# Where the inputs of four convolution pairs are kept: two pairs move from the mixers' pool to the pool that outlives it

## The chip, the cores and the metric

The kernel runs on one core of one Trainium2 chip. The metric is the device time of one launch in microseconds (us), the median of the runs shown. Lower is better. The engines are named as in the profile: PE (TensorE), with PEld for its weight loads, DVE (VectorE), ACT (ScalarE), POOL (GpSimd) and SP (SyncE, which here only issues DMAs).

## The reference, cut to what matters

One decoder layer on a sequence of 1024 positions with 1024 channels, all in float32. The part that matters here is the Conformer branch and what runs beside it:

```python
def conformer_branch(u_glu, dw_w, dw_b, ln_g, ln_b, w_out):
    a, g = jnp.split(u_glu, 2, axis=-1)
    v = a * jax.nn.sigmoid(g)
    v = causal_dwconv(v, dw_w, dw_b)          # 31 taps, each channel by itself
    v = jax.nn.silu(layer_norm(v, ln_g, ln_b))
    return v @ w_out
...
    y_a = conformer_branch(...)
    y_b = ssd_branch(...)
    h = LN(alpha*h + (sigmoid(gate_a)*y_a + sigmoid(gate_b)*y_b) @ w_o)
    h = LN(alpha*h + conv_ffn(h))
```

The convolution at a position needs the 30 positions before it, so the end of the first half of the sequence is needed again at the start of the second.

## The kernel before, in words

The sequence is worked through in two halves of 512 positions (`hh` 0 and 1). Each half runs `mixers(hh)`, then `combine(hh)`, then an output projection; the feed-forward part follows for both halves together. Activations lie with channels on the 128 partitions, so a tile of 128 channels and 512 positions is one matmul wide.

**Products in three parts.** Every float32 product is three matmuls on rounded parts (`mm3`, lines 183 to 185): high weights by high input, high weights by low input, low weights by high input. `project` (line 187) does this for 8 slices of 128 input channels, 24 matmuls for one output tile. `weights` (line 144) brings the weights: SP loads 512 KB into a tile `st` (line 147, 3 buffers), ACT casts it to the high part of `w` (line 149, 3 buffers), and DVE subtracts to get the low part (line 154, called the split below). The first matmuls of line 183 and 184 need only the cast; line 185 needs the split.

**mixers(hh)** has four groups. In each group `glu` (line 434) makes two tiles `v` of the convolution's input, `v = a * sigmoid(g)` with 30 columns of the previous half in front (line 443 copies them from `v_halo`; line 446 saves the end of the half there). Then `conv31` (line 449) works on the pair: ACT makes the start value `c` (line 455), and DVE adds 30 taps for each tile, one SCALAR_TENSOR_TENSOR each (line 466). Group g has the tiles i = 2g and 2g+1: the first pair is v0 and v1, the fourth v6 and v7. The taps have the lowest priority (`high_priority(offset=-1500)`), so the taps of the fourth pair are done during `combine`. `c` of the first six is stored to DRAM; c6 and c7 stay in the memory of the core.

**combine(hh)** does eight rounds. Each round has a projection for the second gate (`gate`, weights `w_gb`, sigmoid on ACT in line 739) and one for the second half of the state-space output (`w_sp`), with `mb = (ya + ps) * gb` on DVE (lines 759 and 760; `ya` is loaded by SP in line 750 as `yb`). On PE the order is gb0, gb1, sp0, gb2, sp1, gb3, sp2, gb4 and so on. Beside that the layer norm of the convolution's output is made: POOL sums the eight `c` (lines 699 and 701), a float32 matmul with `mean_w` gives the mean (line 706, in `deviations`), DVE subtracts it (line 708), ACT squares, POOL sums (line 714), a second such matmul gives the variance (line 718).

**What sets the order.** Nobody writes the order of an engine's instructions by hand. A scheduler orders them at build time by priority and by its own model of when an instruction could run and when a tile's memory is free. Once built, each engine takes its instructions in that order and waits on semaphores. So a change of where a tile lies can change the order around it.

**Pools.** `statep` ("states") is opened before the first half and closed after the second `combine`. `pl` in `mixers` is opened anew for each half, and the pool of `combine` takes over its memory when it closes. The tiles `v` lie in `pl`, with 4 buffers; v4 takes the place of v0, and v6 that of v2.

Of the kernel before, what the change touches and what calls it, by code (L numbers as in the profile page):

```python
# [8 lines left out]
F32 = mybir.dt.float32  # L9
# [7 lines left out]
P = 128  # L17
D = 1024
T = 1024
HALF = 512  # L20
# [3 lines left out]
KC = 31  # L24
# [31 lines left out]
def kernel(  # L56
# [18 lines left out]
    def pool(name, bufs=1, **kw):  # L75
        return tc.tile_pool(name=name, bufs=bufs, reuse_waits="tile", **kw)
# [11 lines left out]
    def bank(which):  # L88
        n_ps[0] += 1
        pl, tag = (pacc, "acc") if which else (psm, "sm")  # L90
        return pl.tile([P, 512], F32, tag=tag, name=f"{tag}{n_ps[0]}")
# [4 lines left out]
    statep = state_stack.enter_context(pool("states", side="right"))  # L96
# [65 lines left out]
    def col_weights(hh, ct):  # L162
        scr = low_scr.get(ct)
        return weights(
            wcol[ct], f"c{hh}_{ct}", None if hh else scr, scr if hh else None
        )
# [20 lines left out]
    def project(ps, w, xs):  # L187
        for k in range(KD):
            mm3(
                ps,  # L190
                lambda i: w[:, i, k * P : (k + 1) * P],
                lambda i: xs[:, i, k, :],
                k == 0,
                k == KD - 1,
            )
# [238 lines left out]
    def glu(pl, hh, hT, i):  # L434
        pa, pg = bank(1), bank(1)
        wa = col_weights(hh, CT_A + i)
        project(pa, wa, hT)
        wg = col_weights(hh, CT_G + i)
        project(pg, wg, hT)
        v = pl.tile([P, HALF + KC - 1], F32, tag="v", bufs=4, name=f"v{hh}_{i}")  # L440
        s = pl.tile([P, HALF], F32, tag="sig", name=f"sig{hh}_{i}")
        A.activation(out=s, in_=pg, func=AF.Sigmoid)
        A.copy(v[:, : KC - 1], v_halo[:, i, :])
        V.tensor_mul(v[:, KC - 1 :], pa, s)
        if hh == 0:
            A.copy(v_halo[:, i, :], v[:, HALF:])
        return v
# [195 lines left out]
    def mixers(hh, hT):  # L643
        pre = first_columns(hh, hT, (CT_B, CT_C, CT_X))
        with pool(f"mixers{hh}") as pl:
            time_steps(pl, hh, pre[0])
            scaled = parts = None
            for g in range(GROUPS):
                BT = conv4(pl, hh, column(hh, hT, CT_B + g) if g else pre[1], 16 + g)
                CT = conv4(pl, hh, column(hh, hT, CT_C + g) if g else pre[2], 20 + g)  # L650
                xT = pl.tile([P, 4, HALF], F32, tag="x4", bufs=2, name=f"x4_{hh}_{g}")
                for i in range(4):
                    j = 4 * g + i
                    conv4(pl, hh, column(hh, hT, CT_X + j) if j else pre[3], j, xT[:, i, :])
                zs = z_gate(pl, hh, hT, g)
                vs = [(i, glu(pl, hh, hT, i)) for i in (2 * g, 2 * g + 1)]
                if g:
                    scaled()
                if g == 1:
                    yT = big_tile(f"yT{hh}_0")  # L660
                if g in (1, 2):
                    parts(yT)
                split_2 = parts
                scaled, parts = ssd_group(pl, hh, g, xT, BT, CT, zs)
                if g == 3:
                    ssm_out_first(pl, hh, yT)
                    yT = big_tile(f"yT{hh}_2")
                    split_2(yT)
                    gate_first(pl, hh, hT, range(3))
                    scaled()  # L670
                    parts(yT)
                with tc.high_priority(offset=-1500):
                    accs = conv31(pl, hh, vs)
            gate_first(pl, hh, hT, range(3, 8))
# [531 lines left out]
    mixT, _ = combine(1, hT, yT, accs)  # L1206
# [122 lines left out]
```

## Time and profile before

| what | value |
|---|---|
| three runs | 1958.3, 1958.61, 1961.29 us; median 1958.61 us |
| the profiled execution | 1960.26 us, its span 1958.4 us |
| granted PE clock, mean over the span | 0.997 |
| PE busy | 1929.1 us, 99% of the span |
| DVE busy | 1599.8 us, 82% |
| ACT busy | 1081.2 us, 55% |
| POOL busy | 218.9 us, 11% |

The span is the part of the profiled execution between its first and last instruction; 1.86 us of its time lie outside. A row of the timeline reads: start in us from the span's start, duration, engine, line, operation, output<-inputs, shape, count, and in brackets how long the engine sat idle just before and what released it. Rows of equal instructions that follow each other are merged, so a row x11 lasts from its start to the end of the eleventh. Names in the profile have no buffer numbers: `w_gb` is any of the gates' weight tiles.

### The profile page before, as it was taken

The page shows a single profiled execution, that of the slowest core. Times are in us where ns is not written, and L with a number is a line of the kernel's source. Part 1 is how long each engine was busy: PE and PEld are TensorE (multiplying, and loading weights), DVE is VectorE, ACT ScalarE, POOL GpSimd, SP SyncE. Part 2 cuts the span into 40 slices and gives each one's busy share as a digit, 9 for nine tenths or more (in the row PEclk, how much of TensorE's full clock was granted, in tenths as well). Part 3 has the DMA queues.
Part 4 walks back from the last instruction along what each step waited for, and adds up shares of the span by engine and source line. Part 5 has one row for each costly group of instructions (what it writes and reads, how often), then busy time and mean ns, then how long its engine had stood idle before and what let it go on. Part 6 is the DMA issues. An engine that isn't in the chain of part 4 may idle for free.

```text
span 1958.4 us, 25837 instructions
## 1 busy us (share of the span) xinstructions
PE 1929.1 (99%) x9453; PEld 1574.9 (80%) x9453; DVE 1599.8 (82%) x2224; ACT 1081.2 (55%) x1615; POOL 218.9 (11%) x258
## 2 busy tenths in 40 slices
PE   9999999999999999999999999999999999989997
PEld 8888878788788788888878888888888888867886
DVE  7599999999786538898999546587788888879778
ACT  4676767653263266777765435365555555544432
POOL 0001010112210001111112140010000000121010
PEclk9999999999999999999999999999999999999999
DMA  7645555447355565556545644566455455588673
GB/s 270 224 166 205 174 202 185 159 171 245 116 188 212 198 214 175 205 181 208 176 159 168 216 145 134 188 237 230 163 167 189 166 188 178 198 301 276 195 230 127
DMA packets 127648, 378.36 MB, mean 193 GB/s; under 512 B 15104, under 2 KB 15648, under 8 KB 127520
## 3 DMA queue, kind: packets, MB, share of 16 engines
q1 hardware_dynamic: 107424, 318.48, 48.2%
q0 software_dynamic: 13760, 46.69, 6.9%
q10 hardware_dynamic: 6336, 11.54, 1.6%
q8 instruction: 74, 1.21, 0.3%
q14 instruction: 54, 0.44, 0.1%
HBM read 289.99 MB, written 86.65 MB: 192 GB/s over the span
## 4 chain that ended last, share of the span: by engine, by line
PE 60%; DVE 10%; DMA 3%; ACT 2%; issue 2%; DVEq 0%; SPq 0%; ACTq 0%
PE acc L185 13%; PE acc L184 13%; PE acc L183 13%; PE sm L184 6%; PE sm L185 6%; PE sm L183 6%; DVE c L466 4%; DMA dr<-wdown 1%; DVE x L421 1%; DMA st_wo<-wo 1%; DMA b_scr<-fo 1%; PE sm L551 1%; PE sm L554 0%; DVE m L546 0%; ACT m L519 0%
## 5 line engine op out<-in xcount | busy, mean ns | idle before, releaser
L183 PE MATMUL acc<-hT,w_c 128*128 128x512 f32 x1000 | 391.2, 391 | 0.0
L185 PE MATMUL acc<-hT,w_c 128*128 128x512 f32 x1000 | 391.1, 391 | 0.0
L184 PE MATMUL acc<-hT,w_c 128*128 128x512 f32 x1000 | 391.0, 391 | 0.0
L466 DVE SCALAR_TENSOR_TENSOR c<-v,pc,c 128x512 f32<-128x512 f32 x480 | 369.7, 798 | 7.3 <-ACT c L455 4.5
L183 PEld LDWEIGHTS acc<-hT,w_c 128*128 128x128 f32 x1000 | 187.8, 188 | 40.6 <-issue 1.9
L185 PEld LDWEIGHTS acc<-hT,w_c 128*128 128x128 f32 x1000 | 187.8, 188 | 40.0 <-issue 1.5
L184 PEld LDWEIGHTS acc<-hT,w_c 128*128 128x128 f32 x1000 | 187.8, 188 | 39.5 <-issue 1.1
L149 ACT CAST w_c<-st_c 128x1024 fp32r<-128x1024 f32 x128 | 133.9, 1046 | 127.6 <-PE acc L185 100.6
L530 POOL TENSOR_TENSOR ce<-ce,xbc 128x1024 f32<-128x1024 f32 x28 | 82.2, 2936 | 681.7 <-ACT ce L529 681.7
L1116 ACT CAST w_dn<-dr 128x1024 fp32r<-128x1024 f32 (+1 forms) x73 | 68.6, 944 | 88.3 <-DMA dr<-wdown 36.7
L183 PE MATMUL sm<-h1s,w_s 128*128 128x512 f32 x264 | 102.7, 389 | 0.0
L184 PE MATMUL sm<-h1s,w_s 128*128 128x512 f32 x264 | 102.7, 389 | 0.0
L185 PE MATMUL sm<-h1s,w_s 128*128 128x512 f32 x264 | 102.2, 389 | 0.0
L519 ACT ACTIVATE m<-ab,acs 128x128 f32<-128x128 f32 x256 | 78.3, 390 | 37.7 <-PE sm L551 36.6
L154 DVE TENSOR_TENSOR w_c<-st_c,w_c 128x1024 fp32r<-128x1024 f32 x64 | 79.4, 1243 | 22.3 <-ACT w_c L149 17.1
L1117 DVE TENSOR_TENSOR w_dn<-dr,w_dn 128x1024 fp32r<-128x1024 f32 (+1 forms) x73 | 78.9, 1092 | 6.1 <-ACT w_dn L1116 6.1
L421 DVE SCALAR_TENSOR_TENSOR x<-u,pc,x 128x512 f32<-128x512 f32 x96 | 78.8, 835 | 3.9 <-ACT x L419 3.8
L185 PE MATMUL acc<-h1b,w_ue 128*128 128x512 f32 x176 | 68.8, 394 | 0.3 <-DVE w_ue L154 0.3
L183 PE MATMUL acc<-h1b,w_ue 128*128 128x512 f32 x176 | 68.7, 390 | 0.0
L184 PE MATMUL acc<-h1b,w_ue 128*128 128x512 f32 x176 | 68.5, 389 | 0.0
L183 PE MATMUL sm<-h1b,w_s 128*128 128x512 f32 x176 | 68.5, 389 | 0.0
L184 PE MATMUL sm<-h1b,w_s 128*128 128x512 f32 x176 | 68.5, 389 | 0.0
(325 smaller groups left out, 4547.3 us busy)
## 6 DMA issues: line engine op xcount, KB each, us to landing
st_c<-wcol SPq DMA_DIRECT2D x128, 512.0 KB, 4.4
low_scr<-w_c SPq DMA_DIRECT2D x64, 512.0 KB, 2.9
w_c<-low_scr SPq DMA_DIRECT2D x64, 512.0 KB, 4.4
ab<-acs_scr SPq DMA_DIRECT2D x32, 512.0 KB, 4.1
dr<-wdown SPq DMA_DIRECT2D x55, 256.0 KB, 5.2
st_wo<-wo SPq DMA_DIRECT2D x24, 512.0 KB, 4.5
st_ue<-wup SPq DMA_DIRECT2D x22, 512.0 KB, 3.6
first_scr<-first ACTq DMA_DIRECT2D x44, 256.0 KB, 3.0
```

What stands on the lines that cost most here:

```text
L149: casts.append(A.copy(w[:, 0, :], st))
L154: V.tensor_tensor(out=w[:, 1, :], in0=st, in1=w[:, 0, :].bitcast(F32), op=ALU.subtract)
L183: TE.matmul(ps, wa(0), xa(0), start=start, stop=False, skip_group_check=more)
L184: TE.matmul(ps, wa(0), xa(1), start=False, stop=False, skip_group_check=more)
L185: TE.matmul(ps, wa(1), xa(0), start=False, stop=stop, skip_group_check=more)
L421: V.scalar_tensor_tensor(out=o, in0=u[:, k : k + HALF], scalar=pc[:, wc + k : wc + k + 1], in1=o, op0=ALU.mult, op1=ALU.add,)
L466: V.scalar_tensor_tensor(out=accs[i], in0=v[:, k : k + HALF], scalar=pc[:, wc + k : wc + k + 1], in1=accs[i], op0=ALU.mult, op1=ALU.add,)
L519: A.activation(out=m[:, h, :], in_=ab[:, h, :], func=AF.Relu, scale=-1.0, bias=acs[:, c, 8 * g + h : 8 * g + h + 1],)
L530: G.tensor_tensor(out=ce, in0=ce, in1=CT[:, cs].unsqueeze(1).to_broadcast([P, 8, P]), op=ALU.mult)
L551: TE.matmul(o, xs[:, h * HP : (h + 1) * HP], m[:, h, :], start=True, stop=first)
L1116: A.copy(w[:, 0, cs], src)
L1117: V.tensor_tensor(out=w[:, 1, cs], in0=src, in1=w[:, 0, cs].bitcast(F32), op=ALU.subtract)
```

## The change

The tiles `v` of the second and fourth pair (i = 2, 3, 6, 7) are taken from `statep` with 2 buffers, those of the first and third pair (0, 1, 4, 5) from `pl` with 2 buffers. The number of tiles and all arithmetic stay. v6 still takes the place of v2. What is new is that v6 and v7 no longer lie in memory that `combine` takes over, and that v2 and v3 of the second half take the places of v6 and v7 of the first.

```diff
-        v = pl.tile([P, HALF + KC - 1], F32, tag="v", bufs=4, name=f"v{hh}_{i}")
+        v = (statep if i & 2 else pl).tile(
+            [P, HALF + KC - 1], F32, tag="v", bufs=2, name=f"v{hh}_{i}"
+        )
```

All lines behind these stand two further down in the changed kernel (line 466 becomes 468, line 706 becomes 708, line 154 stays).

On POOL the order of instructions is the same; on the other engines it differs in few places. The first is DVE in `combine` of the first half, from the split of sp1's weights on. `c_6` and `c_7` are the convolution's sums of the fourth pair, `w_gb_3`, `w_sp_2`, `w_gb_4` the weights of the next projections. Before:

```order
L154 TENSOR_TENSOR w_sp_1_4622<-st_sp_1_4620,w_sp_1_4622 128x1024
L466 SCALAR_TENSOR_TENSOR c_6_4222<-v_6_3506,pc,c_6_4222 128x512
L466 SCALAR_TENSOR_TENSOR c_7_4224<-v_7_3574,pc,c_7_4224 128x512 x10
L154 TENSOR_TENSOR w_gb_3_4654<-st_gb_3_4652,w_gb_3_4654 128x1024
L759 TENSOR_TENSOR mb_0_4528<-yb_0_4526,acc_4553 128x512
L154 TENSOR_TENSOR w_sp_2_4688<-st_sp_2_4686,w_sp_2_4688 128x1024
L760 TENSOR_TENSOR mb_0_4528<-mb_0_4528,gb_0_4492 128x512
L759 TENSOR_TENSOR mb_1_4529<-yb_1_4617,acc_4619 128x512
```

The same place on DVE in the changed kernel:

```order
L154 TENSOR_TENSOR w_sp_1_4622<-st_sp_1_4620,w_sp_1_4622 128x1024
L468 SCALAR_TENSOR_TENSOR c_6_4222<-v_6_3506,pc,c_6_4222 128x512
L468 SCALAR_TENSOR_TENSOR c_7_4224<-v_7_3574,pc,c_7_4224 128x512 x2
L761 TENSOR_TENSOR mb_0_4528<-yb_0_4526,acc_4553 128x512
L468 SCALAR_TENSOR_TENSOR c_7_4224<-v_7_3574,pc,c_7_4224 128x512
L762 TENSOR_TENSOR mb_0_4528<-mb_0_4528,gb_0_4492 128x512
L154 TENSOR_TENSOR w_gb_3_4654<-st_gb_3_4652,w_gb_3_4654 128x1024
L468 SCALAR_TENSOR_TENSOR c_7_4224<-v_7_3574,pc,c_7_4224 128x512 x4
L154 TENSOR_TENSOR w_sp_2_4688<-st_sp_2_4686,w_sp_2_4688 128x1024
L468 SCALAR_TENSOR_TENSOR c_7_4224<-v_7_3574,pc,c_7_4224 128x512 x3
L761 TENSOR_TENSOR mb_1_4529<-yb_1_4617,acc_4619 128x512
```

Seven of the ten taps of c7 moved behind the split of `w_gb_3`, and three of these behind that of `w_sp_2`; the sum and the product of `mb_0` moved ahead of the split of `w_gb_3`.

The second place is ACT in the same stage. `v_2_7066` and `v_3_7131` are tiles of the second half; in the kernel before, their copies of line 443 stand some 90 rows later, at the start of the second `mixers`. Before:

```order
L149 CAST w_sp_1_4622<-st_sp_1_4620 128x1024
L739 ACTIVATE gb_0_4492<-acc_4462 128x512
L149 CAST w_gb_3_4654<-st_gb_3_4652 128x1024
L739 ACTIVATE gb_1_4524<-acc_4494 128x512
L149 CAST w_sp_2_4688<-st_sp_2_4686 128x1024
L739 ACTIVATE gb_2_4615<-acc_4585 128x512
L149 CAST w_gb_4_4745<-st_gb_4_4743 128x1024
```

The same place on ACT in the changed kernel:

```order
L741 ACTIVATE gb_0_4492<-acc_4462 128x512
L149 CAST w_sp_1_4622<-st_sp_1_4620 128x1024
L741 ACTIVATE gb_1_4524<-acc_4494 128x512
L445 COPY v_2_7066<-v_halo 128x30
L149 CAST w_gb_3_4654<-st_gb_3_4652 128x1024
L149 CAST w_sp_2_4688<-st_sp_2_4686 128x1024
L741 ACTIVATE gb_2_4615<-acc_4585 128x512
L445 COPY v_3_7131<-v_halo 128x30
L149 CAST w_gb_4_4745<-st_gb_4_4743 128x1024
```

Two copies now stand ahead of casts. The first waits for the last tap of c6, which is the last reader of v6; the second for the last tap of c7.

The third place is PE in the same stage; `sm_4717` is the mean of the convolution's sums, `acc_4742` the projection gb4. One piece of the difference (- before, + changed):

```order
 L184 MATMUL acc_4685<-yT_2_4096,w_sp_2_4688 128x512
 L185 MATMUL acc_4685<-yT_2_4096,w_sp_2_4688 128x512
+L708 MATMUL sm_4717<-stats_4461,mean_w 128x512
 L183 MATMUL acc_4742<-hT_338,w_gb_4_4745 128x512
 L184 MATMUL acc_4742<-hT_338,w_gb_4_4745 128x512
@@ -2061,5 +2062,4 @@
 L183 MATMUL acc_4742<-hT_338,w_gb_4_4745 128x512
 L184 MATMUL acc_4742<-hT_338,w_gb_4_4745 128x512
-L706 MATMUL sm_4717<-stats_4461,mean_w 128x512
 L185 MATMUL acc_4742<-hT_338,w_gb_4_4745 128x512
 L183 MATMUL acc_4742<-hT_338,w_gb_4_4745 128x512
```

The mean's matmul moved from inside the projection gb4, where 20 of its 24 matmuls stood ahead of it, to the front of it.

Besides these: the matmul of the variance moved three matmuls forward, from inside the projection gb6 to the front of it; the loads of `yb` for mb0 and mb1 moved on SP ahead of the loads of gb3's, sp2's and gb4's weights; on DVE, four of the subtractions of line 708 moved ahead of the split of `w_gb_5`; some squares of line 713 moved on ACT against casts; and the copies of line 443 for v2 and v3 of the first half moved to the very start of ACT's instructions, where a load of an activation table now stands ahead of them. No other instruction moved.

## The prediction

> **What bounds the kernel now.** I read the page's engine rows first, then PE's waits, then the timeline around the longest of them.
>
> ```profile
> span 1958.4 us, 25837 instructions
> PE 1929.1 (99%) x9453; PEld 1574.9 (80%) x9453; DVE 1599.8 (82%) x2224; ACT 1081.2 (55%) x1615; POOL 218.9 (11%) x258
> ```
>
> PE is busy for 99% of the span. So only two things can shorten the kernel: fewer or faster matmuls, or a wait of PE that goes. The change leaves the matmuls alone. Two rows of PE's waits (us in total, times, longest):
>
> ```profile
> PE acc L185 <- DVE w_gb L154: 4.2, 1, 4.2
> PE sm L551 <- DVE m L546: 2.7, 2, 2.5
> ```
>
> The longest single wait of the kernel, 4.2 us, is on a split of gate weights, and it happens once. It lies in the first `combine`, on PE:
>
> ```profile
> 499.39 0.39 PE L183 MATMUL acc<-yT,w_sp 128*128 128x512 f32 x1
> 504.83 0.39 PE L183 MATMUL acc<-hT,w_gb 128*128 128x512 f32 x1
> 505.06 0.39 PE L184 MATMUL acc<-hT,w_gb 128*128 128x512 f32 x1
> 509.67 0.80 PE L185 MATMUL acc<-hT,w_gb 128*128 128x512 f32 x1 [4.22 <-DVE w_gb L154]
> 517.12 0.39 PE L183 MATMUL acc<-yT,w_sp 128*128 128x512 f32 x1
> ```
>
> From 499.39 to 504.83 a projection of 24 matmuls takes 5.44 us, a step of 0.227 us each. The third matmul of gb3, the first that needs the low weights, was due at 505.06 + 0.23 = 505.29 and starts at 509.67: **4.38 us** lost. The 22 steps from there to the next projection at 517.12 take 7.45 us in place of 22 x 0.227 = 4.99: another **2.46 us**. The table of stretches says why (PE busy, then the granted clock):
>
> ```profile
> 505.00:507.80 2.80, 0.44 (x2) 1.00 0.00 0
> 507.80:509.60 1.80, 0.00 (x0) 0.50 0.00 0
> 509.60:514.60 5.00, 4.93 (x12) 0.50 0.75 255
> 514.60:520.00 5.40, 5.40 (x25) 1.00 0.49 154
> ```
>
> The clock drops to half at about 507.8, in the wait, and stays there to 514.6. The place costs 4.38 + 2.46 = 6.84 us in all. What PE waits for stands on DVE:
>
> ```profile
> 497.94 1.22 DVE L154 TENSOR_TENSOR w_sp<-st_sp,w_sp 128x1024 fp32r<-128x1024 f32 x1
> 499.07 9.41 DVE L466 SCALAR_TENSOR_TENSOR c<-v,pc,c 128x512 f32<-128x512 f32 x11
> 508.39 1.22 DVE L154 TENSOR_TENSOR w_gb<-st_gb,w_gb 128x1024 fp32r<-128x1024 f32 x1
> 509.53 0.68 DVE L759 TENSOR_TENSOR mb<-yb,acc 128x512 f32<-128x512 f32 x1
> 511.75 0.68 DVE L760 TENSOR_TENSOR mb<-mb,gb 128x512 f32<-128x512 f32 x1
> 500.52 1.66 DVE L466 SCALAR_TENSOR_TENSOR c<-v,pc,c 128x512 f32<-128x512 f32 x1
> 503.00 0.75 DVE L466 SCALAR_TENSOR_TENSOR c<-v,pc,c 128x512 f32<-128x512 f32 x1
> ```
>
> The split of `w_gb_3` stands behind eleven taps, one of c6 and ten of c7. The last two rows are single taps out of the eleven. The split ends at 508.39 + 1.22 = 509.61; PE starts 0.06 us later.
>
> **The change, part by part.**
>
> *Taps behind the split.* By the order, DVE now runs the tap of c6, two taps of c7, the sum of `mb_0`, one tap, the product of `mb_0`, and then the split. The second tap of c7 is the row at 500.52 and ends at 502.18. Then come 0.68 + 0.75 + 0.68 = 2.11 us, the split starts at 504.29, ends at 505.51, and PE starts at 505.57 where it was due at 505.29. A rest of 0.28 us stays. Neighbouring rows overlap a little (509.53 + 0.68 is past the next start), so the rest could be zero. **Gain: 4.38 - 0.28 = 4.10 us.**
>
> *The clock.* A wait of 2.52 us elsewhere left the clock at full:
>
> ```profile
> 997.14 0.44 PE L551 MATMUL sm<-m,xs 128*64 128x128 f32 x4 [2.52 <-DVE m L546]
> 994.50:997.10 2.60, 0.12 (x1) 0.00 (x0) 1.63 (x3) 2.59 (x4) 0.00 (x0) 1.00 0.80 312
> 997.10:1000.50 3.40, 3.36 (x38) 2.99 (x39) 3.40 (x7) 3.37 (x6) 0.00 (x0) 1.00 0.73 241
> ```
>
> So a rest of 0.28 us should leave it there too: **gain 2.46 us**, in all 6.56. The Trainium skill, page "TensorE: Matmul & The Clock Gate", section "HAM oscillation — how this bites in real kernels", prices such a drop at half of the throttled time. By that the 6.8 us at half clock would be an estimated 3.4 us, and the gain 7.5. The rows give less, since PE sat idle for 1.9 of the 6.8 us, and I keep the rows.
>
> *The copies on ACT.* ACT is in order, so what stands behind the copy of v2 (the casts of `w_gb_3` and `w_sp_2`) waits for c6's last tap. The row of ACT's cast for gb3 before, the group of copies (ns, min/median/max), and POOL's last two sums:
>
> ```profile
> 494.15 1.06 ACT L149 CAST w_gb<-st_gb 128x1024 fp32r<-128x1024 f32 x1 [3.89 <-PE acc L185]
> L443 ACT COPY v<-v_halo x16: 198/226/234, 27.4 to 920.0; 128x30 f32<-128x30 f32 x16
> 499.96 1.67 POOL L701 TENSOR_TENSOR stats<-stats,c 128x512 f32<-128x512 f32 x1 [8.93 <-DVE c L466]
> 508.62 2.12 POOL L701 TENSOR_TENSOR stats<-stats,c 128x512 f32<-128x512 f32 x1 [6.99 <-DVE c L466]
> ```
>
> c6's tap ends at 499.07 + 0.75 = 499.82, the copy near 500.1, the cast of `w_gb_3` near 501.2: 6 us later than before, but 3 us ahead of 504.29, when DVE comes to the split, and ahead of PE's 504.83. Cost nothing; without that cover it would be 1:1. The copy of v3 waits for c7's last tap: 505.51, four taps at 0.79 (eight took 502.18 to 508.48), a split of 1.22, three taps: 512.3. Cast of `w_gb_4` by 513.6; its split follows the two `mb_1` steps, by 515 (by 516 if it takes 2.3 us beside POOL). PE reaches gb4 at 505.57 + 22 x 0.227 + 5.44 = 516.0 and needs the low weights a matmul of the mean (1 us) later. Cost nothing.
>
> *The mean's matmul.* It needs POOL's sum with c7, 2.12 us after c7's last tap: 512.3 + 0.14 + 2.12 = 514.5. In front of gb4 PE comes to it at 516.0. Margin 1.5 us. The 20 matmuls that stood ahead of it (4.5 us) are gone as cover, so a later sum would cost 1:1. Then the subtractions start 11 us earlier than before, and the split of `w_gb_5` moves behind four of them: DVE has room, as it sat idle here:
>
> ```profile
> 518.41 1.22 DVE L154 TENSOR_TENSOR w_sp<-st_sp,w_sp 128x1024 fp32r<-128x1024 f32 x1 [3.52 <-ACT w_sp L149]
> 528.16 3.68 DVE L708 TENSOR_TENSOR cc<-cc,sm 128x512 f32<-128x512 f32 x6 [2.85 <-PE sm L706]
> 543.41 0.56 POOL L289 DMA_DIRECT2D in_sq<-gin  x1 [0.30 <-POOL stats L714]
> 545.89 1.02 PE L718 MATMUL sm<-stats,mean_w 128*128 128x512 f32 x2
> ```
>
> POOL's last sum of squares ended 0.3 us before 543.41, 15 us after 528.16. From 517 that is 532, and PE comes to the variance at about 538.6 (545.89 less the gain and three matmuls). Cost nothing.
>
> *Loads on SP.* The two `yb` loads now go ahead of the load of `st_gb_3`:
>
> ```profile
> 480.14 0.43 SPq L641 DMA_DIRECT2D g_scr<-gt  x1
> 486.52 0.33 SPq L147 DMA_DIRECT2D st_gb<-wcol  x1
> 499.61 0.85 SPq L750 DMA_DIRECT2D yb<-y_scr  x2
> ```
>
> SP is free from 480.6 to 486.5, and issuing both takes 0.85 us. Nothing queues behind them.
>
> *The start.* ACT gets a table load and two copies ahead of its first square root:
>
> ```profile
> 0.80 1.28 ACT L239 ACT_TABLE_LOAD   x1 [0.80 <-PEq L1316]
> 1.91 0.29 POOL L116 MEMSET v_halo<- 128x240 f32 x1
> 6.00 0.29 ACT L239 ACTIVATE rs_in<-mv_in,eps 128x1 f32<-128x1 f32 x1 [3.92 <-DVE mv_in L238]
> ```
>
> The load ends at 2.08, `v_halo` is ready at 2.2, two copies take 0.45, a second load 1.28: done by 4.0, with 2 us of idle time left before 6.00. Cost nothing.
>
> *The sum.* 6.56 us off the profiled execution's 1960.26 gives 1953.70, span 1951.84. That execution stands 1.65 us above the median of 1958.61. If none of these 1.65 lie in this wait, the median falls to 1952.05; if all do, the median run has only 4.91 to give, and 1953.70 stays. I take **1952.5**, nearer to the first: two of the three runs lie within 0.3 us of each other, so the 1.65 may as well be of the profiled execution as a whole. What is late next is the same split, by 0.28 us.
>
> **The rivals.**
>
> *The clock still drops.* If DVE is slower here, the rest grows. Rows for it: a tap took 1.66 us beside POOL's sum, and a split took 2.31 beside POOL at 484.18, `mb` 1.07 at 535.92:
>
> ```profile
> 484.18 2.31 DVE L154 TENSOR_TENSOR w_sp<-st_sp,w_sp 128x1024 fp32r<-128x1024 f32 x1
> 535.92 1.07 DVE L760 TENSOR_TENSOR mb<-mb,gb 128x512 f32<-128x512 f32 x1
> ```
>
> With those prices on all four steps the split ends 2.8 us later, the wait is 3.1 us, and with a drop of the clock the gain is 6.84 - 3.08 - 2.46 = 1.3: **1957.3**. It decides where the wait passes about 2.5 us, where the clock fell in the row above. The same page, section "Part 1: The HAM clock gate", lets the clock fall only after an idle window of about 3.4 us, by which this rival would need a still longer wait; in this trace it fell 2.5 us in, so I go by the trace. Against it: POOL's sum ends at 501.63, before these steps. Chance 0.09.
>
> *The gain is given back.* If a later stage runs at the pace of DVE or ACT, PE only waits there instead: **1958.6**. For it: in the second `mixers` PE has the 2.52 us wait above. Against it: that is all it has there, and DVE's waits right behind the place (3.52, 2.85) end on ACT and PE, which both come earlier. Chance 0.07.
>
> *Slower: PE held by the mean.* Seven taps of c7 now lie between the split and the mean, which stands in front of gb4. Their group:
>
> ```profile
> L466 DVE SCALAR_TENSOR_TENSOR c<-v,pc,c x480: 656/750/2912, 95.8 to 1094.1; 128x512 f32<-128x512 f32 x160
> ```
>
> At the longest of 2.912 us seven taps take 20.4 in place of 5.5 us. The sum is 14.9 late, less the margin of 1.5 leaves a wait of 13.4, and the clock drops (2.46): 15.9 lost against 6.56 gained, **1968.0**. Once the clock drops, 4.10 of the gain are left, so it decides for slower where the seven taps cost over 1.5 + 4.10 us more than 5.5, about 1.6 us each. Against it: the median is 0.75, and POOL is idle in that stretch. Chance 0.04.
>
> **How the numbers follow.** My forecast, with the wait gone and the gain kept, has 0.80. All its values gain more than 3.9 us, which is 0.2% and about what a measurement of this kernel can tell from no change: faster 0.80. The first two rivals are within it: same 0.16. Slower 0.04. Low end: 6.84 off the fastest run, 1958.3, is 1951.5, less 1 us for runs that scatter by 3: 1950.5. High end: the first rival's 1957.3. What is left out above, give-back and held mean, has 0.11.
>
> **What would show it.** Right: PE's wait on `w_gb` gone from the top of its waits, or under 0.5 us; the clock at 1.00 through 505 to 520; sp2 starting near 510.6 in place of 517.12; only one split between seven taps and the mean; a span of 1951 to 1953. The copy steps are wrong if a cast of `w_gb` waits on DVE and PE behind it. The mean step is wrong if PE shows a wait on POOL at line 708. The whole is wrong if sp2 starts early and the span stays: then a new wait of PE after 520 names the place.

## The result, and the profile after

| | before | after |
|---|---|---|
| median | 1961.29 us | 1955.61 us |
| lowest to highest, 9 runs each | 1958.3 to 1967.26 us | 1952.82 to 1958.13 us |
| the profiled execution, its span | 1960.26 us, 1958.4 us | 1952.82 us, 1951.1 us |

The ratio is 0.997, with a 95% interval of 0.9961 to 0.9978. So the changed kernel is 0.3% faster: by the ratio 5.9 us of 1961, between 4.3 and 7.6 (the two medians lie 5.7 apart). The profiled execution after is the fastest of its nine. The three runs of before that the prediction worked with were the first of these nine.

The engine rows of the changed kernel's page:

```profile
span 1951.1 us, 25836 instructions
PE 1928.4 (99%) x9453; PEld 1574.6 (81%) x9453; DVE 1599.3 (82%) x2224; ACT 1082.7 (55%) x1616; POOL 217.6 (11%) x258
```

No engine has less to do than before; ACT has one table load more. The span is 7.3 us shorter because PE waits less: it is idle for 22.7 us in place of 29.3, and busy for 0.7 us less. PE's longest waits in the changed kernel (us in total, times, longest):

```profile
PE acc L184 <- DVE w_dn L1119: 2.9, 3, 1.5
PE sm L553 <- DVE m L548: 2.7, 2, 2.5
PE sm L257 <- POOL ident masks.py:199: 1.7, 1, 1.7
PE acc L183 <- ACT w_dn L1118: 1.5, 2, 1.1
PE sm L184 <- DVE w_dn L1119: 1.1, 1, 1.1
```

The wait of 4.2 us on `w_gb` is gone. The place itself on PE's timeline, from gb3 to the variance:

```profile
504.69 0.39 PE L183 MATMUL acc<-hT,w_gb 128*128 128x512 f32 x1
505.18 0.50 PE L185 MATMUL acc<-hT,w_gb 128*128 128x512 f32 x1
510.30 0.39 PE L183 MATMUL acc<-yT,w_sp 128*128 128x512 f32 x1
515.75 1.02 PE L708 MATMUL sm<-stats,mean_w 128*128 128x512 f32 x2
516.20 0.79 PE L183 MATMUL acc<-hT,w_gb 128*128 128x512 f32 x1
538.39 1.02 PE L720 MATMUL sm<-stats,mean_w 128*128 128x512 f32 x2
```

The third matmul of gb3, due two steps after 504.69 at 505.15, starts at 505.18: 0.03 us lost where it was 4.38. From gb3's first row to sp2's first row it is 5.61 us; the 24 steps take 5.44 undisturbed, so 0.17 us are lost where 6.85 were. The place has given 6.7 us. Neither the mean (515.75) nor the variance (538.39) shows a wait. DVE at the same place:

```profile
502.05 0.68 DVE L761 TENSOR_TENSOR mb<-yb,acc 128x512 f32<-128x512 f32 x1
502.65 0.74 DVE L468 SCALAR_TENSOR_TENSOR c<-v,pc,c 128x512 f32<-128x512 f32 x1
503.31 0.68 DVE L762 TENSOR_TENSOR mb<-mb,gb 128x512 f32<-128x512 f32 x1
503.91 1.21 DVE L154 TENSOR_TENSOR w_gb<-st_gb,w_gb 128x1024 fp32r<-128x1024 f32 x1
505.05 3.10 DVE L468 SCALAR_TENSOR_TENSOR c<-v,pc,c 128x512 f32<-128x512 f32 x4
508.07 1.22 DVE L154 TENSOR_TENSOR w_sp<-st_sp,w_sp 128x1024 fp32r<-128x1024 f32 x1
509.20 2.32 DVE L468 SCALAR_TENSOR_TENSOR c<-v,pc,c 128x512 f32<-128x512 f32 x3
```

The split starts at 503.91 and ends at 505.12. The prediction had 504.29 and 505.51. Each row starts 0.07 to 0.09 us before the one above it has ended: from the sum of `mb_0` to the split it is 1.86 us where the durations add up to 2.10. That is most of the 0.38 us, and so the rest of 0.28 us, which the prediction allowed might be zero, was 0.03. ACT, and POOL's sums:

```profile
499.79 0.22 ACT L445 COPY v<-v_halo 128x30 f32<-128x30 f32 x1 [9.68 <-DVE c L468]
499.92 1.05 ACT L149 CAST w_gb<-st_gb 128x1024 fp32r<-128x1024 f32 x1
511.56 0.22 ACT L445 COPY v<-v_halo 128x30 f32<-128x30 f32 x1 [9.15 <-DVE c L468]
511.68 1.05 ACT L149 CAST w_gb<-st_gb 128x1024 fp32r<-128x1024 f32 x1
```

```profile
511.67 1.30 POOL L703 TENSOR_TENSOR stats<-stats,c 128x512 f32<-128x512 f32 x1 [10.09 <-DVE c L468]
```

ACT stands idle for 9.68 and 9.15 us behind the two copies, and PE loses nothing by it: the first cast ends at 500.97, about 3 us before DVE comes to its split. The sum for the mean ends at 512.97, 2.8 us before PE needs it; the margin had been put at 1.5, with a sum of 2.12 us in place of 1.30.

The stretch around the place, in before and then in the changed kernel (us, busy us and count of PE, PEld, DVE, ACT, POOL; granted clock; DMA share; GB/s):

```profile
475.00:545.00 70.00, 65.78 (x279) 53.58 (x278) 56.48 (x59) 22.14 (x30) 24.32 (x16) 0.95 0.42 139
```

```profile
475.00:545.00 70.00, 70.00 (x306) 57.08 (x305) 61.16 (x63) 25.42 (x36) 23.52 (x16) 1.00 0.48 162
```

PE fills all 70 us and does 27 matmuls more in them, at full clock. The next 155 us, in before and then in the changed kernel:

```profile
545.00:700.00 155.00, 155.00 (x719) 126.32 (x718) 109.34 (x167) 70.63 (x104) 4.29 (x8) 1.00 0.58 201
```

```profile
545.00:700.00 155.00, 155.00 (x729) 126.36 (x728) 107.15 (x171) 70.55 (x105) 4.29 (x8) 1.00 0.58 198
```

PE stays full in both, so the gain isn't given back there.

### The profile page after: what moved, and what is told of

The parts are those of the page before. It is cut to its first block, busy times and chain, and to the rows that moved or that the text cites. A ratio compares the mean times of both kernels' runs of the same rounds, so it can differ in the third digit from the quotient of the medians.

```text
span 1951.1 us, 25836 instructions
## 1 busy us (share of the span) xinstructions
PE 1928.4 (99%) x9453; PEld 1574.6 (81%) x9453; DVE 1599.3 (82%) x2224; ACT 1082.7 (55%) x1616; POOL 217.6 (11%) x258
## 4 chain that ended last, share of the span: by engine, by line
PE 90%; DVE 5%; DMA 3%; ACT 1%; issue 1%; SPq 0%; POOL 0%; DVEq 0%; ACTq 0%
PE acc L185 21%; PE acc L183 21%; PE acc L184 21%; PE sm L184 6%; PE sm L185 6%; PE sm L183 6%; PE sm L553 2%; PE sm L561 1%; PE sm L556 1%; DMA dr<-wdown 1%; PE sm L514 1%; DMA b_scr<-fo 1%; DVE c L468 0%; PE acc L402 0%; DVE x L421 0%
```

## The experiments

All kernels here compute the whole reference. Times are medians; the ratio is to the kernel before, run on the same chip (1960.68 us in the first four experiments, 1960.47 in e5 to e8, 1960.44 in e9 and e10). Diffs are against the changed kernel. `issue_after(a, b)`, a helper of the kernel, makes the scheduler put a behind b on their engine.

My theory: the gain comes from DVE's order alone, and the pools matter only because they make the scheduler choose it. The rival: the memory itself brings it, since v6 and v7 no longer lie where `combine` takes over, or since early copies or loads help.

**e1: the new pools, with DVE's order of before.**

```diff
+                if hh == 0 and j == 3:
+                    issue_after(los[-1], tap[0, 7, KC - 2])
+                    issue_after(first_mb[0], los[-1])
...
+                if hh == 0 and j == 2:
+                    issue_after(los[-1], first_mb[0])
+                    issue_after(first_mb[1], los[-1])
```

`los[-1]` is the split just issued, `tap[0, 7, KC - 2]` the last tap of c7, `first_mb` the steps of `mb_0`. A further line keeps sp2's matmuls behind gb3's on PE.

> The changed kernel with the tiles where the change put them, but DVE made to follow the order of the kernel before at the one place: ten taps of c7, then the split of w_gb_3, then mb_0. Theory (the order of DVE at this place is the whole gain): PE waits about 4.2 us on the split again, the clock drops to half behind it, and the time is that of the kernel before within 0.1% (ratio 0.999 to 1.001). Rival (the place of the tiles in memory, or the mean and the copies that moved with them, bring the gain): ratio about 0.997, as the changed kernel.

Measured: 1961.04 us, ratio 1.0002 (0.9993 to 1.001). PE's timeline at the place:

```profile
505.70 0.39 PE L184 MATMUL acc<-hT,w_gb 128*128 128x512 f32 x1
510.61 0.79 PE L186 MATMUL acc<-hT,w_gb 128*128 128x512 f32 x1 [4.29 <-DVE w_gb L155]
518.16 0.39 PE L184 MATMUL acc<-yT,w_sp 128*128 128x512 f32 x1
```

gb3 began at 505.70 and sp2 at 518.16, so 12.46 - 5.44 = 7.02 us were lost, wait and clock together. The copies on ACT stay where the change put them (the first at 500.78, ahead of gb3's cast), and so does the mean (523.61, in front of gb4). With the memory of the change and the order of before, the whole gain is gone, to within 0.1%. So the memory alone doesn't bring it, and neither do the copies or the mean by themselves: the rival falls. The opposite trial, the pools of before with DVE's order of the change, was not run, so it isn't shown that the order would bring the gain without the new memory.

**e2: the mirror.** The first and third pair go to `statep`, the second and fourth stay in `pl`; nothing else changes, and DVE keeps its order of before.

```diff
-        v = (statep if i & 2 else pl).tile(
+        v = (pl if i & 2 else statep).tile(
```

> The mirror of the change: first and third pair in the pool that outlives the mixers, second and fourth in the mixers' pool. As many bytes change pools, but DVE keeps the order of the kernel before at the place. Theory: the 4.2 us wait stays, ratio 0.999 to 1.001. Rival (the smaller mixers' pool or the shifted addresses bring it): ratio about 0.997.

Measured: 1961.72 us, ratio 1.0009 (0.9999 to 1.0018). PE's timeline, and the stretches from the wait to sp2:

```profile
509.89 0.74 PE L185 MATMUL acc<-hT,w_gb 128*128 128x512 f32 x1 [4.13 <-DVE w_gb L154]
```

```profile
505.50:510.00 4.50, 0.37 (x3) 0.11 (x1) 4.36 (x7) 0.89 (x1) 1.15 (x1) 1.00 0.00 0
510.00:513.40 3.40, 3.40 (x8) 2.65 (x9) 3.37 (x5) 0.00 (x0) 0.97 (x1) 0.50 0.71 238
```

The same wait stands, and 6.04 us are lost at the place. As many tiles moved between the pools, and no gain: it matters which pairs move. That fits the theory: the taps that stand ahead of the split are those of the fourth pair. The clock's part was 1.75 us here and not 2.46, because the drop came only at 510.0, after the wait had ended, and lasted 3.4 us, half as long as in before.

**e3 and e4: three and five of the seven taps back ahead of the split.** This sets the wait to sizes between 0 and 4.4 us, to price the place and find where the clock falls.

```diff
+                if hh == 0 and j == 3:
+                    issue_after(los[-1], tap[0, 7, 25])
```

In e4 the number is 27 in place of 25.

> The changed kernel with three of the seven taps put back ahead of the split of w_gb_3. The split ends 3 x 0.775 = 2.3 us later, so PE waits 2.3 us there. If the clock stays at full after so short a wait, 2.3 of the 6.6 us of gain are lost in the trace and the ratio is about 0.998; if it drops, 4.8 are lost and the ratio is about 0.9993.

> The same with five of the seven taps put back: PE waits 3.9 us. If the drop of the clock is a price of its own, it comes here: 3.9 + 2.5 us lost, nearly the whole gain, ratio about 1.000. If the clock stays, 3.9 us lost, ratio about 0.9988.

Measured, e3: 1957.13 us, ratio 0.9981 (0.9972 to 0.999). e4: 1958.4 us, ratio 0.9987 (0.9978 to 0.9996). PE's timeline of e3, then of e4:

```profile
507.74 0.50 PE L186 MATMUL acc<-hT,w_gb 128*128 128x512 f32 x1 [1.67 <-DVE w_gb L155]
```

```profile
505.30 0.39 PE L184 MATMUL acc<-yT,w_sp 128*128 128x512 f32 x1
508.90 0.79 PE L186 MATMUL acc<-hT,w_gb 128*128 128x512 f32 x1 [2.98 <-DVE w_gb L155]
```

Three taps cost 1.97 us at the place and no clock; 1.8 of it is wait. Five cost 4.78: 3.1 of wait, and 1.7 because the clock was at half for 3.4 us from 508.7. Both waits were shorter than the 2.3 and 3.9 us that I had expected. In these executions DVE came to the returned taps 1.2 and 1.0 us ahead of gb3's first row, where in the changed kernel it comes to the split 0.78 us ahead. In e4 the scheduler also put two matmuls of sp2 (the row at 505.30 is the first) in front of the awaited one. Medians rise with the taps, 1955.6, 1957.1, 1958.4, 1961.0 for none, three, five and all: the order sets the time in steps, as the theory has it.

**e5: the copies without their early place.** The two copies of the second half are issued behind the one of v0, back in the second `mixers`.

```diff
+        halo[hh, i] = A.copy(v[:, : KC - 1], v_halo[:, i, :])
+        if hh and i in (2, 3):
+            issue_after(halo[hh, i], halo[1, 0])
```

> The changed kernel, but the two copies into the second half's v2 and v3 stand at the start of the second mixers again, as before the change; nothing else moves. The prediction costed their new place at nothing: the cast of w_gb_3 goes back to about 494 us, and DVE comes to its split no sooner. Ratio to the kernel before that of the changed kernel, 0.997, and the same PE start of the split's matmul near 505.2. Rival (ACT standing still behind the copies costs something): ratio lower than the changed kernel's by 0.0005 or more.

Measured: 1956.46 us, ratio 0.998 (0.9971 to 0.9988). The cast and the split of gb3's weights, and gb3's first row on PE:

```profile
495.08 1.05 ACT L150 CAST w_gb<-st_gb 128x1024 fp32r<-128x1024 f32 x1 [3.90 <-DVE w_gb L155]
```

```profile
505.01 1.21 DVE L155 TENSOR_TENSOR w_gb<-st_gb,w_gb 128x1024 fp32r<-128x1024 f32 x1
```

```profile
505.79 0.39 PE L184 MATMUL acc<-hT,w_gb 128*128 128x512 f32 x1
```

The cast has its old place again: it starts 10.7 us ahead of gb3's first row, as in before (494.15 and 504.83), and not 4.8 us as in the changed kernel. DVE's split starts 0.78 us ahead of that row, in the changed kernel too (503.91 against 504.69), and 0.16 us are lost, as against 0.17. The copies cost nothing at this place, and bring nothing. The median lies 1.2 us above that of e8, which ran beside it, but the intervals overlap.

**e6: the mean back inside gb4**, with 18 of its 24 matmuls ahead of it (before had 20).

```diff
+                if hh == 0 and j == 4:
+                    issue_after(means[0], mms[-3])
```

> The changed kernel, but the mean's matmul stands inside the projection gb4 again, with 20 matmuls ahead of it. The prediction gave its new place a margin of 1.5 us and no cost: ratio that of the changed kernel, 0.997, no wait of PE at this place either way. Rival (an earlier mean is part of the gain, by earlier subtractions and squares): ratio 0.998 or more.

Measured: 1952.39 us, ratio 0.9966 (0.9953 to 0.9978). The mean's matmul starts at 519.90 without a wait, and 0.2 us are lost at the place. The interval overlaps that of the change, so the mean's new place costs nothing that could be measured.

**e7 and e9: what is late next.** The longest single wait left is that on `m`, the decay factors of the second `mixers`, 2.5 us. In e7 the exponential of line 528 goes ahead of a Silu on ACT, in e9 ahead of one exponential of `ce` too.

```diff
+            if hh and g == 3 and i == 1:
+                issue_after(silu, exps[-1])
...
+                if (hh, g, c) == (1, 2, 3):
+                    issue_after(ce_exp, exps[-1])
```

The last two lines are e9's.

> The changed kernel with one more row moved: at about 986 us ACT does the exponential of m ahead of a silu of the next group, which saves two loads of an activation table (1.28 us each) and brings the exponential forward by about 3.2 us. PE's longest wait of the changed kernel, 2.5 us on m, stands behind it. If such a wait is worth its full length: 2.5 us less than the changed kernel, ratio to the kernel before about 0.9957. If it is given back later: 0.997.

> E7 with the exponential of m also ahead of that of ce in the same chunk, another 1 us forward. If PE's wait on m is worth its length: the wait falls from 2.5 us in the changed kernel (1.5 in E7) to about 0.5, and with it the place where the clock drops in some executions is gone: 2 us less than the changed kernel, and up to 3.6 where the clock had dropped; ratio to the kernel before about 0.996. If it is given back: as the changed kernel, 0.997.

Measured, e7: 1954.58 us, ratio 0.9966 (0.9954 to 0.9977). e9: 1953.45 us, ratio 0.9964 (0.9952 to 0.9976). PE's waits in e7 and in e9:

```profile
PE sm L558 <- DVE m L553: 1.6, 2, 1.5
```

```profile
PE acc L185 <- DVE w_dn L1126: 5.3, 4, 1.6
PE sm L563 <- POOL ce L539: 1.1, 1, 1.1
PE sm L560 <- DVE m L555: 0.2, 1, 0.2
```

e7 took only 1.1 of the 2.5 us: the `ce` exponential, a table load and a cast were still ahead of it on ACT. e9 left 0.2 us of the wait on `m`, and a wait of 1.1 us on `ce` came in its place. Both medians lie 1 to 2 us below the change's, but the intervals overlap widely. Whether they are better than the change is not settled; both are faster than before.

**e8 and e10: the changed kernel again**, for its scatter and its clock.

> The changed kernel itself, beside the three others on the same chip: ratio 0.9961 to 0.9978, and the same PE rows at 505 us in a second profile.

> The changed kernel beside it on the same chip: ratio 0.996 to 0.998, a wait of 2.5 us on m near 990 us, with or without a drop of the clock behind it.

Measured, e8: 1955.31 us (1949.42 to 1958.59), ratio 0.9972 (0.9961 to 0.9983). e10: 1955.44 us (1953.8 to 1958.23), ratio 0.9979 (0.9969 to 0.9988). The gain repeats, and so does the place: in e8 gb3 starts at 504.78 and sp2 at 510.39, again 5.61 us. The clock does not repeat: the same wait on `m`, in the profile of the result and in e10, each with its timeline row, the next row of line 183, and the stretch behind the wait:

```profile
990.32 0.44 PE L553 MATMUL sm<-m,xs 128*64 128x128 f32 x4 [2.54 <-DVE m L548]
992.55 0.39 PE L183 MATMUL acc<-hT,w_c 128*128 128x512 f32 x1
```

```profile
990.40:994.00 3.60, 3.60 (x40) 3.12 (x41) 3.60 (x8) 3.59 (x6) 0.00 (x0) 1.00 0.82 284
```

```profile
991.71 0.44 PE L553 MATMUL sm<-m,xs 128*64 128x128 f32 x4 [2.52 <-DVE m L548]
995.56 0.39 PE L183 MATMUL acc<-hT,w_c 128*128 128x512 f32 x1
```

```profile
992.00:995.50 3.50, 3.50 (x33) 3.15 (x29) 3.50 (x8) 3.49 (x6) 0.00 (x0) 0.52 0.85 298
```

From the end of the wait to that matmul it is 2.23 us in the one and 3.85 in the other, so the drop cost 1.6 us. The wait was the same.

## Why the prediction was right, step by step

- **Taps behind the split: right.** The wait fell from 4.38 to 0.03 us; 4.10 had been put down, 4.35 came. e1 shows the cause: with DVE's order of before, the wait is back at 4.29 us and the gain is nil.
- **The clock: right at this place.** It stays at 1.00 (the stretch above), and the 2.46 us are gone. But the row on which that step leant, a wait of 2.52 us that left the clock at full, was luck: the same wait dropped it in five of the ten profiles that have it at that length. The step itself didn't hang on it, since only 0.03 us of wait came.
- **The copies, the mean: right**, shown by e5 and e6. The loads on SP and the start cost nothing that the trace shows: no wait on `yb`, and none at the start that is new. They were not tried apart.
- **The sum.** 6.56 us were forecast for the profiled execution, and 6.7 came at the place. Its span fell by 7.3. What else differs shows in before's waits on `w_dn`, and in a stretch late in the changed kernel:

```profile
PE acc L184 <- DVE w_dn L1117: 3.7, 3, 1.6
PE sm L184 <- DVE w_dn L1117: 2.1, 1, 2.1
PE acc L183 <- ACT w_dn L1116: 2.1, 2, 1.1
```

```profile
1722.70:1726.10 3.40, 3.40 (x10) 2.62 (x9) 2.60 (x3) 0.33 (x2) 0.51 (x1) 0.50 0.00 0
```

  These waits are 2.4 us longer in all than the changed kernel's 2.9, 1.1 and 1.5. Against that the changed kernel has a clock drop there that before has not, worth about 1.6 us (ten matmul steps take 3.98 us from 1722.36, and the same ten 2.42 in before). That leaves 0.8, about the 0.6 by which the span fell more than the place gave. Both lie in the feed-forward part, which the change doesn't touch. The three waits come to between 4.7 us (e7) and 8.0 (e9) over all twelve profiles, and e9 has the change, so I take them for scatter. Against the median the forecast was 6.1 of 1958.6, and the measurement gave 5.9 (4.3 to 7.6). The absolute forecast of 1952.5 lies 3 us under the median of after, since the nine runs of before have a median 2.7 us above that of the first three.
- **The rivals.** No clock drop at the place: DVE ran no slower here than its medians. No give-back: PE is full from 475 to 700 us. No hold by the mean: margin 2.8 us. But the first rival's deciding point, a wait of 2.5 us, was too firm, as the waits on `m` show; and its price of 2.46 us was too high in e4, where a wait of 3.1 us came with 1.7.

That the scheduler chose this order because v6's and v7's memory lasts is read from the built order and from e2; how it weighs such things was not tried.

## What to carry to other kernels

Where PE is busy for 99%, look for its longest single wait, and then at what stands ahead of the awaited instruction on the engine that it waits for: here seven low-priority taps. A change of a tile's pool is judged by the order of instructions that comes out of it; with the order of before put back, the whole 0.3% was gone, and the new memory was worth nothing that e1 could measure. A wait of 2.5 us and more on PE cost about half as much again here, wherever it dropped the clock.

## What the runs showed of the hardware

The length of a wait alone doesn't decide whether the clock drops, and a drop has no fixed price. At the place of the change, PE idle for 4.2, 4.3, 4.1 and 3.0 us (before, e1, e2, e4) dropped it, and 1.7 us (e3) did not; the wait of 2.5 us on `m` dropped it in e3, e5, e6, e8 and e10, and did not in before, after, e1, e2 and e4. The stretches at half clock were about 3.4 us long, or twice that (before and e1). The cost was 2.5 us in before, 1.7 in e2 and e4, 1.6 at `m`. It is about half of that part of the stretch in which PE has work: 4.9 of 6.8 us in before, all 3.4 in e2.

What goes with a drop can be read from the places where the clock changes. In before these are 507.81, 514.64 and 1951.65 us, which lie 2 and 421 steps of 3.413 us apart, and in every profile with more than one change they are whole steps apart. Counted in such steps, these are the stretches around the wait on `m`, in e10 (wait from 989.19 to 991.71) and then in the profile of the result (987.78 to 990.32):

```profile
988.71:992.12 3.41, 0.89 (x11) 0.49 (x11) 2.43 (x3) 3.38 (x5) 0.00 (x0) 1.00 0.75 282
```

```profile
985.44:988.85 3.41, 2.34 (x11) 1.60 (x9) 2.52 (x2) 3.37 (x5) 1.31 (x1) 1.00 0.70 203
988.85:992.26 3.41, 1.95 (x33) 1.80 (x33) 3.32 (x5) 3.38 (x6) 0.00 (x0) 1.00 0.75 265
```

In e10 the whole wait lies in one step, PE is busy for 0.89 of 3.41 us, and the clock falls at the step's end, 992.12. In the profile of the result a step ends inside the wait, PE is busy for more than half of each part, and the clock stays. All ten go this way: the five that dropped have a step in which PE is busy for 26 to 30%, the other five none below 43%. So does the drop at 1722.7 us after the change: no wait there is longer than 1.14 us, but two of them fall for the most part in one step and leave PE busy for 46% of it. The exact limit is not shown: steps with 44 to 52% were followed by a drop in some profiles, and steps with 43 to 52% were not in others.

The Trainium skill, page "TensorE: Matmul & The Clock Gate", section "Part 1: The HAM clock gate", describes a free-running window of 3413 ns and a clock that is set by how busy PE has been recently. The steps above agree with that, and so does the fact that the same wait falls now on one side and now on the other. The page asks for a whole idle window before a drop; here waits of 2.5 and 3.0 us were enough.

Such drops seem to make a part of the 3 us by which runs of one kernel differ. The granted clock of every run is on record, to 0.001, which is about one step at half clock. Of the 26 runs of the changed kernel (the result, e8 and e10), the six at 0.995 and 0.996 have a mean of 1956.9 us, the four at 0.998 and 0.999 one of 1953.5. But the sixteen at 0.997 alone reach from 1952.8 to 1958.1 us, so a good part of the scatter has another cause, which stays open.
